# A squared-ReLU channel sub-layer: square with one operand from PSUM, plain sums in both halves, one gate near the end

## The chip, the cores and the metric

The kernel runs on one core of a Trainium2 chip, in one launch. The metric is device time in microseconds (us) of that launch. The kernel before takes 2147.57 us, the median of three runs (2147.03, 2147.57 and 2153.73).

## What is computed

One step of a decoder trunk with one layer, width D = 1024, in fp32: a prompt of 1024 rows and a sample of 8 rows share the weights. The layer has a mixer sub-layer (paged attention over a cache, gated linear attention) and a channel sub-layer. The change lies in the channel sub-layer of the prompt. For a block of rows `x1` with its modulated form `h`:

```
h   = ln(x1) * (1 + scale) + shift                # scale, shift from c
u   = h @ w_ff1                                   # 1024 x 4096
mlp = relu(u)**2 @ w_ff2                          # 4096 x 1024
y   = layer_norm(ALPHA * x1 + gate * mlp) * ln2_g + ln2_b
```

`gate` is one row of 1024 values for all rows of the prompt.

## The kernel before

The work is written as generators (flows) that yield between pieces; a planner picks the order in which instructions reach each engine, from the order of the flows, their lags and its own costs. Each engine then works through its own list strictly in order. The order around the change is thus nobody's single choice, and one changed instruction can move its neighbours on every engine.

The prompt is done in two halves of 512 rows, by `ffn(0, h2a, False)` and then `ffn(1, h2b, True)`; the second one also carries the 8 sample rows. At its start, the first runs beside the end of the paged attention of the sample (loads `kt`, `vt` by POOL, products and sums on `kt` at L659 and L661 by DVE, matmuls `va` by PE) and the norms (`xr`) of the second half's mixer.

A half has 32 units of 128 hidden columns. For each unit `up` does 24 matmuls into one of two PSUM tiles `pmm`. The factor 24 is 8 blocks of the contraction by 3 products: matmul operands are split into a high and a low part (names ending in h and l), and `three` takes high x high, low x high, high x low. Then, per unit, ACT makes `rl = relu(pmm)` (L1502), DVE squares it in place (L1503), ACT copies the high part `hidh` (L313) and DVE subtracts to get `hidl` (L314). Weights come by SP (`wf`, L319), are split by ACT (`wfh`, `wf2h`, L313) and by POOL (`wfl`, `wf2l`, L314).

Units go down in groups of two (the last group of the second half has four). A group makes 8 output tiles of 128x512, 4 row tiles `t` by 2 column halves `cc`. `down_tile` does 6 matmuls (12 for four units) into one of two PSUM tiles `pz` (cc = 0) or one of two `ptr` (cc = 1). `add_up` then brings the PSUM tile into the SBUF sum `f[t][cc]`:

- In the first half, the first group copies (DVE, L1548), later groups add (DVE, L1550). Ahead of the last group the sums are multiplied by the gate (L1614) and `ALPHA * x1`, loaded again as `xf`, is added (L1615).
- In the second half `f` is loaded with `x1` by SP in 8 transfers (L205) during the first group's `up`, and every tile of every group is gated: `tmpf = gate * pz` (L1556), then `f += tmpf` (L1560), or with ALPHA in the first group (L1558).

In both halves the last group's tiles are gated (L1556, L1560), and after each pair the norm follows: statistics on DVE (L299, L301, L304, L1630), scaling by ACT (L1632), `ln2_g` and `ln2_b` by DVE and POOL (L1633, L1634; for the last row tile of all by DVE alone, L1626, L1627), then the store (L1184). The tiles `rl`, `tmpf`, `xf` share one pool of 9 buffers.

The last sample rows (`srow`) are finished by `smp_end` beside the second half's last group.

Of the kernel before, what the change touches and what calls it, by code (L numbers as in the profile page):

```python
# [15 lines left out]
AF = mybir.ActivationFunctionType  # L16
ALU = mybir.AluOpType
# [3 lines left out]
P = 128  # L21
# [5 lines left out]
ALPHA = 2.0 ** 0.25  # L27
# [89 lines left out]
def tile_trunk_step(ctx: ExitStack, tc: tile.TileContext, i: dict, o: dict):  # L117
    nc = tc.nc
    V, S, G, E = nc.vector, nc.scalar, nc.gpsimd, nc.tensor
# [5 lines left out]
    def hk(shape, name, dt=F32):  # L125
        return sb.tile(list(shape), dt, tag="hk", name=name, bufs=N_HK)

    def mid(shape, name, dt=F32):
        return sb.tile(list(shape), dt, tag="mid", name=name, bufs=N_MID)

    def fa(shape, name, dt=F32):
        return sb.tile(list(shape), dt, tag="fa", name=name, bufs=N_FA)
# [22 lines left out]
    def p_mm(shape=(P, 512), name="pmm"):  # L155
        return ps.tile(list(shape), F32, tag="mm", name=name, bufs=2)
# [19 lines left out]
    def mm(out, lhsT, rhs, start, stop, share=1.0, **kw):  # L176

        n = 1
        for x in out.shape[1:]:
            n *= x  # L180
        if lhsT.dtype == F32R:
            tile_, dt = 0, 0.008 + n / 2286.0
        else:
            k, m = (next(x for x in (32, 64, 128) if y <= x) for y in (lhsT.shape[0], out.shape[0]))
            tile_, dt = (k, m) if k * m < P * P else 0, (0.2 + n / 610.0) * m / 128.0

        flow.t += dt * share + (0.1 if tile_ != mode[0] else 0.0)
        mode[0] = tile_
        ins = E.matmul(out, lhsT, rhs, start=start, stop=stop, **kw)  # L189
        flow.last = ins.ins.name  # L190
        flow.times.append(flow.t)
        flow.names.append(flow.last)
        return ins

    def not_before(ins, name):

        tc.add_manual_dep(
            ins.ins, name, mybir.DependencyInfo(mybir.DependencyClass.NoSync, mybir.DependencyReason.DATA),
            reason="not before the rows can be there",
        )  # L200

    def fetch(dst, src, lead):


        ins = nc.sync.dma_start(dst, src)  # L205
        x = bisect(flow.times, flow.t - lead)
        if x:
            not_before(ins, flow.names[x - 1])
# [29 lines left out]
    d_x1 = [tc.dram_tile([P, D], F32, name=f"d_x1{t}") for t in range(8)]  # L238
# [12 lines left out]
    for c in range(2):  # L251
        t = cp.tile([P, 8], F32, name=f"sel2_{c}")
# [59 lines left out]
    def split(src, hi, lo, eng=None):  # L312
        S.activation(hi, src, AF.Copy)  # L313
        (eng or G).tensor_tensor(lo, src, hi.bitcast(F32), ALU.subtract)  # L314
# [15 lines left out]
    def three(terms):  # L330

        out = []
        for a, b in ((0, 0), (1, 0), (0, 1)):
            out += [(x[a], y[b]) for x, y in terms]
        return out
# [814 lines left out]
    def rows(vec, alloc=hk):  # L1150
        out = []
        for h in range(2):
            t = alloc([P, 512], "row")
            nc.sync.dma_start(t, vec[512 * h : 512 * h + 512].partition_broadcast(P))
            out.append(t)
        return out
# [11 lines left out]
    def halves(dram, n, name, alloc=hk):  # L1168
        out = []
        for h in range(2):  # L1170
            t = alloc([n, 512], name)
            fetch(t, dram[:, 512 * h : 512 * h + 512], 0.0)
            out.append(t)
        return out
# [227 lines left out]
    def ffn(n, h2, smpl):  # L1402
# [3 lines left out]
        f = [[fa([P, 512], f"f{t}{h}") for h in range(2)] for t in range(4)]  # L1406
        yield lambda: ("h2", n) in done
        gt_t = (ada_acc, gmt.rearrange("p a b -> p (a b)"))
# [85 lines left out]
        def up(u, wh, wl):  # L1494
            p = p_mm()
            steps = three([(h2[k], (wh[:, k, :], wl[:, k, :])) for k in range(8)])
            for x, (h, wt) in enumerate(steps):
                mm(p, wt, h, start=x == 0, stop=x == 23)
                if x % 6 == 5 and x < 23:
                    yield  # L1500
            rl = hk([P, 512], "rl")
            S.activation(rl, p, AF.Relu)  # L1502
            V.tensor_tensor(rl, rl, rl, ALU.mult)  # L1503
            hid[u][0:2] = mid([P, 512], "hidh", F32R), mid([P, 512], "hidl", F32R)
            split(rl, hid[u][0], hid[u][1], V)
            yield
# [27 lines left out]
        def down_tile(us, ws, t, cc):  # L1534
            tk = slice(P * t, P * t + P)
            p = (p_z, p_tr)[cc]()
            steps = three([
                ((hid[u][0][:, tk], hid[u][1][:, tk]), (ws[x][0][:, cc, :], ws[x][1][:, cc, :]))
                for x, u in enumerate(us)
            ])  # L1540
            for x, (h, wt) in enumerate(steps):
                mm(p, h, wt, start=x == 0, stop=x == len(steps) - 1)
            return p


        def add_up(f, g, p, first):
            if n == 0 and first:
                V.tensor_copy(f, p)  # L1548
            elif n == 0:
                V.tensor_tensor(f, f, p, ALU.add)  # L1550
            else:
                gated(f, g, p, first)

        def gated(f, g, p, first=False):
            tmp = hk([P, 512], "tmpf")
            V.tensor_tensor(tmp, g, p, ALU.mult)  # L1556
            if first:
                V.scalar_tensor_tensor(f, f, ALPHA, tmp, ALU.mult, ALU.add)  # L1558
            else:
                V.tensor_tensor(f, f, tmp, ALU.add)  # L1560

        groups = [list(range(u, u + 2)) for u in range(0, NU, 2)]
        if smpl:
# [1 line left out]
        steps = [(u, None) for u in groups[0]]  # L1565
        for x, us in enumerate(groups[:-1]):
            steps += [(u, None) for u in groups[x + 1][:2]] + [(x, us)]
        us = groups[-1]
        steps += [(u, None) for u in us[2:]] + [(None, us)]

        def load(x, us):
            if us is None:
                return load_up(x)
            return (yield from load_down(us))

        def smp_end():
            yield lambda: summed == [NU // 2, NU // 2]
            part = hk([P, 512], "partf2")
            S.activation(part, pfs[0], AF.Copy)
            xs, gts = sample_rows(d_x1s, d_gate[1][1:9])  # L1580
            yield E_LAG
            for cc in range(2):
                p3 = p_tr([8, 512], "pfs3")
                mm(p3, sel2[cc], part, start=True, stop=True)
                V.tensor_tensor(gts[cc], gts[cc], p3, ALU.mult)
                V.scalar_tensor_tensor(xs[cc], xs[cc], ALPHA, gts[cc], ALU.mult, ALU.add)
            sub_ln(xs, 8, *ln2)
            store(y_s, xs, 8, nc.sync)


        ws = yield from load(*steps[0])
        for y, (x, us) in enumerate(steps[:-1]):
            if smpl and y == len(steps) - 2:
                ln2 = rows(i["ln2_g"][0]), rows(i["ln2_b"][0])
                flow.spawn(smp_end())
            nxt = yield from load(*steps[y + 1])
            if n and steps[y + 1][0] == 0 and steps[y + 1][1] is not None:
                for t in range(4):
                    for h in range(2):
                        fetch(f[t][h], d_x1[4 * n + t][:, 512 * h : 512 * h + 512], 0.0)  # L1600
            if us is None:
                yield from up(x, *ws)
            else:
                for t in range(4):
                    for cc in range(2):
                        add_up(f[t][cc], gt_t[cc], down_tile(us, ws, t, cc), x == 0)
                        yield
            ws = nxt
        us = groups[-1]
        if n == 0:  # L1610
            for t in range(4):
                xs = halves(d_x1[4 * n + t], P, "xf")
                for h in range(2):
                    V.tensor_tensor(f[t][h], f[t][h], gt_t[h], ALU.mult)  # L1614
                    V.scalar_tensor_tensor(f[t][h], xs[h], ALPHA, f[t][h], ALU.mult, ALU.add)  # L1615
        if not smpl:
            ln2 = rows(i["ln2_g"][0]), rows(i["ln2_b"][0])
        g_t, b_t = ln2
# [118 lines left out]
```

## Time and profile before

| | |
|---|---|
| device time, three runs | 2147.03, 2147.57, 2153.73 us |
| the profiled execution | 2144.41 us, span 2142.7 us |
| mean granted TensorE clock | 0.959 of full |
| PE busy | 1962.2 us (92%) |
| DVE busy | 1567.8 us (73%) |
| POOL busy | 909.5 us (42%) |
| ACT busy | 700.2 us (33%) |

Engines: PE is the matrix engine, PEld its weight loads, DVE the vector engine, ACT the scalar engine, POOL the general one, SP issues transfers. Times inside the execution are us from the start of its span. In a row of a timeline, the number in square brackets is the idle time ahead of the instruction on its own engine, and the arrow names what ended it. The channel sub-layer takes the part of the span from about 1205 us to its end. PEclk is the clock granted to PE as a share of full speed.

### The profile page before, as it was taken

Reading aid. Unit: us, or ns where it says so; the run is one execution under the profiler, and the core shown is the slowest. Engines: PE = TensorE matmul, PEld = TensorE weight load, DVE = VectorE, ACT = ScalarE, POOL = GpSimd, SP = SyncE. Lnnn points to the kernel's source line nnn. Section 1 sums busy time; section 2 is a strip of 40 time slices with the busy share of each in tenths; the row PEclk is TensorE's granted clock in tenths of the full one; section 3 lists DMA queues with packets and bytes.
Section 4 is the critical chain, followed back from the end, with each engine's and each line's share of the span. In section 5 each row is a group of like instructions: output and inputs, shape, how many; then the busy total and the mean of one; then the engine's idle time right before and its main releaser. Section 6 shows DMA issues by size and latency. Waiting matters only on the chain.

```text
span 2142.7 us, 29010 instructions
## 1 busy us (share of the span) xinstructions
PE 1962.2 (92%) x11300; PEld 1378.3 (64%) x11300; DVE 1567.8 (73%) x1882; ACT 700.2 (33%) x1136; POOL 909.5 (42%) x615
## 2 busy tenths in 40 slices
PE   5999999998999889879989789999999898999996
PEld 2776755565556656557867556676766666767774
DVE  6578898788777688567897998987436756555656
ACT  2334444543445632222232223223221332122222
POOL 2342243333334323227475647465544533233335
PEclk8999999999999879999999889999999899999998
DMA  7785678787788668898997778888667543442222
GB/s 259 253 300 189 217 244 281 241 280 245 246 277 302 214 205 293 290 340 293 330 312 278 264 258 289 279 279 303 199 216 254 177 158 119 130 136 92 87 83 85
DMA packets 270083, 498.07 MB, mean 232 GB/s; under 512 B 16005, under 2 KB 198629, under 8 KB 234106
## 3 DMA queue, kind: packets, MB, share of 16 engines
q0 software_dynamic: 36864, 268.45, 34.7%
q1 hardware_dynamic: 205538, 199.17, 29.5%
q10 hardware_dynamic: 27544, 28.59, 3.8%
q8 instruction: 89, 1.46, 0.3%
q14 instruction: 48, 0.39, 0.1%
HBM read 465.45 MB, written 30.71 MB: 232 GB/s over the span
## 4 chain that ended last, share of the span: by engine, by line
PE 54%; DVE 20%; DMA 11%; issue 8%; POOL 3%; ACT 3%; SPq 0%; DVEq 0%; ACTq 0%; POOLq 0%
PE pmm L189 20%; PE pz L189 7%; PE ptr L189 7%; PE pbig L189 7%; DMA kt<-in_cache_k,idx 4%; DVE z L661 4%; PE va L189 4%; DVE kt L659 4%; PE pfs L189 2%; DVE kp L772 1%; DMA vt<-in_cache_v,idx 1%; DMA wbr<-in_w_in 1%; DMA wf<-in_w_ff 1%; DVE st L299 1%; DMA ra<-in_w_ada 1%
## 5 line engine op out<-in xcount | busy, mean ns | idle before, releaser
L659 DVE TENSOR_TENSOR kt<-kt,qb 128x2048 f32<-128x2048 f32 x128 | 291.5, 2278 | 73.8 <-DMA kt<-in_cache_k,idx 71.6
L661 DVE TENSOR_REDUCE z<-kt 128x32 f32<-128x2048 f32 x128 | 291.6, 2280 | 1.2
L636 POOL DMA_INDIRECT vt<-in_cache_v,idx x128 | 133.2, 1041 | 309.7 <-PE va L189 133.6
L636 POOL DMA_INDIRECT kt<-in_cache_k,idx x128 | 132.7, 1037 | 283.5 <-DVE z L661 107.9
L314 POOL TENSOR_TENSOR wfl<-wf,wfh 128x1024 fp32r<-128x1024 f32 x64 | 156.4, 2444 | 206.8 <-ACT wfh L313 187.3
L314 POOL TENSOR_TENSOR wf2l<-wf,wf2h 128x1024 fp32r<-128x1024 f32 x62 | 151.3, 2440 | 117.8 <-ACT wf2h L313 105.1
L1503 DVE TENSOR_TENSOR rl<-rl 128x512 f32<-128x512 f32 x64 | 64.5, 1008 | 162.3 <-ACT rl L1502 162.2
L313 ACT ACTIVATE wfh<-wf 128x1024 fp32r<-128x1024 f32 x64 | 67.5, 1055 | 279.5 <-PE ptr L189 152.9
L189 PE MATMUL pmm<-h2h,wfh 128*128 128x512 f32 x512 | 143.9, 414 | 7.6 <-ACT rl L1502 4.3
L189 PE MATMUL va<-vt,wT 128*8 128x512 f32 x1024 | 140.7, 615 | 11.1 <-DMA vt<-in_cache_v,idx 11.0
L189 PE MATMUL pmm<-h2l,wfh 128*128 128x512 f32 x512 | 140.2, 407 | 0.5 <-POOL h2l L314 0.5
L189 PE MATMUL pmm<-h2h,wfl 128*128 128x512 f32 x512 | 133.2, 397 | 0.0
L189 PEld LDWEIGHTS pmm<-h2h,wfh 128*128 128x128 f32 x512 | 95.0, 194 | 51.4 <-issue 21.6
L189 PEld LDWEIGHTS pmm<-h2l,wfh 128*128 128x128 f32 x512 | 96.5, 192 | 31.9 <-issue 10.1
L189 PEld LDWEIGHTS pmm<-h2h,wfl 128*128 128x128 f32 x512 | 95.2, 189 | 27.2 <-issue 6.8
L1560 DVE TENSOR_TENSOR f<-f,tmpf 128x512 f32<-128x512 f32 x120 | 110.4, 943 | 1.2
L189 PE MATMUL pz<-wf2h,hidh 128*128 128x512 f32 x248 | 86.5, 414 | 21.4 <-ACT wf2h L313 10.8
L772 DVE TENSOR_TENSOR_SCAN kp<-kp,zcol 128x512 f32<-128x512 f32 (+3 forms) x96 | 99.7, 1051 | 3.6 <-ACT kp L765 2.5
L1502 ACT ACTIVATE rl<-pmm 128x512 f32<-128x512 f32 x64 | 38.2, 596 | 175.8 <-PE pmm L189 172.8
L189 PE MATMUL pz<-wf2l,hidh 128*128 128x512 f32 x248 | 83.9, 407 | 6.1 <-POOL wf2l L314 6.0
L314 DVE TENSOR_TENSOR hidl<-rl,hidh 128x512 fp32r<-128x512 f32 x64 | 75.0, 1172 | 16.8 <-ACT hidh L313 15.7
L189 PE MATMUL ptr<-wf2h,hidh 128*128 128x512 f32 x248 | 84.4, 408 | 2.0 <-DVE f L1550 1.6
(432 smaller groups left out, 4298.6 us busy)
## 6 DMA issues: line engine op xcount, KB each, us to landing
wf<-in_w_ff SPq DMA_DIRECT2D x128, 512.0 KB
ra<-in_w_ada SPq DMA_DIRECT2D x24, 1024.0 KB
wfs<-in_w_ff SPq DMA_DIRECT2D x20, 512.0 KB
wbr<-in_w_in SPq DMA_DIRECT2D x16, 512.0 KB
d_br<-brg ACTq DMA_DIRECT2D x32, 256.0 KB
g<-d_br SPq DMA_DIRECT2D x32, 256.0 KB
wo<-in_w_o SPq DMA_DIRECT2D x16, 512.0 KB
xt<-in_x_prompt SPq DMA_DIRECT2D x8, 512.0 KB
```

The source lines that it names most:

```text
L189: ins = E.matmul(out, lhsT, rhs, start=start, stop=stop, **kw)
L299: V.bn_stats(st[:n, h, :], xs[h][:n])
L313: S.activation(hi, src, AF.Copy)
L314: (eng or G).tensor_tensor(lo, src, hi.bitcast(F32), ALU.subtract)
L636: G.indirect_dma_start(t, None, src, bass.IndirectOffsetOnAxis(ap=idx[:, 16 * b + j : 16 * b + j + 1], axis=0))
L659: dot = V.tensor_tensor(k3, k3, qb[:, None, :].to_broadcast([P, 4, 512]), ALU.mult)
L661: V.tensor_reduce(z[:, :, :, j], kt.rearrange("p (r h d) -> p r h d", r=4, h=8), AX.X, ALU.add)
L772: V.tensor_tensor_scan(kp[:, 0:w][:, ::-1], kp[:, 0:w][:, ::-1], zcol.to_broadcast([P, w]), init, ALU.mult, ALU.max)
L1502: S.activation(rl, p, AF.Relu)
L1503: V.tensor_tensor(rl, rl, rl, ALU.mult)
L1560: V.tensor_tensor(f, f, tmp, ALU.add)
```

## The change

In three places:

1. The square takes one operand straight from PSUM: `relu(p) * p` instead of `relu(p) * relu(p)`. `pmm` is now released by DVE (L1503), where before ACT (L1502) released it.
2. In both halves the first group's tile is copied to `f` by ACT, and later groups are added by one DVE instruction.
3. In both halves gate and `ALPHA * x1` come once, ahead of the last group. The 8 transfers of `x1` into `f` in the second half go away; 8 transfers `xf` come at its end.

```diff
             S.activation(rl, p, AF.Relu)
-            V.tensor_tensor(rl, rl, rl, ALU.mult)
+            V.tensor_tensor(rl, rl, p, ALU.mult)
...
-        def add_up(f, g, p, first):
-            if n == 0 and first:
-                V.tensor_copy(f, p)
-            elif n == 0:
+        def add_up(f, p, first):
+            if first:
+                S.activation(f, p, AF.Copy)
+            else:
                 V.tensor_tensor(f, f, p, ALU.add)
-            else:
-                gated(f, g, p, first)
-
-        def gated(f, g, p, first=False):
+
+        def gated(f, g, p):
             tmp = hk([P, 512], "tmpf")
             V.tensor_tensor(tmp, g, p, ALU.mult)
-            if first:
-                V.scalar_tensor_tensor(f, f, ALPHA, tmp, ALU.mult, ALU.add)
-            else:
-                V.tensor_tensor(f, f, tmp, ALU.add)
+            V.tensor_tensor(f, f, tmp, ALU.add)
...
-            if n and steps[y + 1][0] == 0 and steps[y + 1][1] is not None:
-                for t in range(4):
-                    for h in range(2):
-                        fetch(f[t][h], d_x1[4 * n + t][:, 512 * h : 512 * h + 512], 0.0)
...
         us = groups[-1]
-        if n == 0:
-            for t in range(4):
-                xs = halves(d_x1[4 * n + t], P, "xf")
-                for h in range(2):
-                    V.tensor_tensor(f[t][h], f[t][h], gt_t[h], ALU.mult)
-                    V.scalar_tensor_tensor(f[t][h], xs[h], ALPHA, f[t][h], ALU.mult, ALU.add)
+        for t in range(4):
+            xs = halves(d_x1[4 * n + t], P, "xf")
+            for h in range(2):
+                V.tensor_tensor(f[t][h], f[t][h], gt_t[h], ALU.mult)
+                V.scalar_tensor_tensor(f[t][h], xs[h], ALPHA, f[t][h], ALU.mult, ALU.add)
```

Below the edit, lines have new numbers: the gated pair of the last group is L1554 and L1555, the gate block L1604 (multiply) and L1605 (with ALPHA), the norm L1616 to L1624. All instructions ahead of the first half's first group keep their order.

First place, SP's list at the first half's start, where `wf_10665` and `wf_10671` are the first group's two down weights and `x` is the second half's rows for the modulation (lines with - are before, with + after):

```order
 L319 DMA wf<-in_w_ff 128x8x128 x2
 L319 DMA wf_10665<-in_w_ff 128x1024
+L319 DMA wf_10671<-in_w_ff 128x1024
+L319 DMA wf<-in_w_ff 128x8x128
 L1381 DMA x_10783<-d_x_126 128x512
 L1381 DMA x_10786<-d_x_127 128x512
 L1381 DMA x_10789<-d_x_128 128x512
 L1381 DMA x_10792<-d_x_129 128x512
-L319 DMA wf_10671<-in_w_ff 128x1024
-L319 DMA wf<-in_w_ff 128x8x128 x2
+L319 DMA wf<-in_w_ff 128x8x128
```

The second down weight and one more weight now stand ahead of the four loads of `x`. On DVE at the same place one `hidl` (L314) now stands ahead of a product on `kt` (L659), where it stood behind it.

Second place, ACT's list at the start of the second half's first group, where `wf2h<-wf_13647` is the split of that group's second down weight:

```order
 L313 ACTIVATE hidh<-rl 128x512
 L1334 ACTIVATE partu<-pups 128x256
-L1502 ACTIVATE rl<-pmm 128x512
 L313 ACTIVATE wf2h<-wf_13647 128x1024
-L313 ACTIVATE hidh<-rl 128x512
+L1502 ACTIVATE rl<-pmm 128x512
+L313 ACTIVATE hidh<-rl 128x512
+L1548 ACTIVATE f_13498<-pz 128x512
```

The split of the weight no longer stands behind the `relu` of a later unit, and the first of the new copies follows.

Third place, DVE's list at the end of the program, from the last unit's `hidl` to the first tile of the last group. Before:

```order
L314 TENSOR_TENSOR hidl<-rl,hidh 128x512
L1585 TENSOR_TENSOR srow<-srow,pfs_16749 8x512
L1585 TENSOR_TENSOR srow<-srow,pfs_16753 8x512
L1586 SCALAR_TENSOR_TENSOR srow<-srow 8x512 x2
L299 BN_STATS st<-srow 8x6 x2
L1556 TENSOR_TENSOR tmpf<-ada_acc,pz 128x512
```

and after:

```order
L299 BN_STATS st<-srow 8x6 x2
L1605 SCALAR_TENSOR_TENSOR f_13498<-xf,f_13498 128x512
L301 BN_AGGR mv<-st 8x2
L1605 SCALAR_TENSOR_TENSOR f_13499<-xf,f_13499 128x512
L304 RECIPROCAL rs<-rs 8x1
L1605 SCALAR_TENSOR_TENSOR f_13500<-xf,f_13500 128x512
L1162 SCALAR_TENSOR_TENSOR nm<-mv,rs 8x1
L1605 SCALAR_TENSOR_TENSOR f_13501<-xf,f_13501 128x512
L1605 SCALAR_TENSOR_TENSOR f_13502<-xf,f_13502 128x512
L1165 TENSOR_TENSOR srow<-srow,row 8x512 x2
L1605 SCALAR_TENSOR_TENSOR f_13503<-xf,f_13503 128x512
L1166 TENSOR_TENSOR srow<-srow,row 8x512
```

Two more L1605 and then L1554, the first gated product, follow. All 8 instructions L1605 thus stand between the statistics of `srow` and the first tile of the last group; the 8 multiplications L1604 stand further ahead, among the tiles of the group before.

## Rows read from the trace of the kernel before

**Rows 1.** Busy time of the engines in stretches of the span (the view of stretches): for each stretch its bounds and length in us, then busy us and, in brackets, the number of instructions of PE, PEld, DVE, ACT and POOL, the granted clock of PE, the DMA share and GB/s.

```profile
1200.00:1250.00 50.00, 41.44 (x167) 29.27 (x167) 48.12 (x61) 15.80 (x27) 29.96 (x19) 0.82 0.62 211
1250.00:1300.00 50.00, 43.49 (x194) 29.37 (x193) 49.23 (x47) 12.73 (x17) 26.94 (x18) 0.93 0.85 298
1400.00:1450.00 50.00, 48.71 (x228) 35.78 (x226) 44.27 (x38) 12.62 (x16) 29.31 (x18) 1.00 0.83 291
...
1550.00:1600.00 50.00, 50.00 (x240) 35.06 (x237) 17.64 (x26) 11.68 (x15) 23.51 (x15) 1.00 0.58 201
...
1650.00:1700.00 50.00, 39.87 (x165) 29.14 (x166) 42.76 (x59) 18.89 (x28) 28.64 (x14) 0.89 0.62 188
...
2000.00:2050.00 50.00, 50.00 (x272) 36.89 (x271) 28.72 (x44) 13.30 (x17) 19.97 (x8) 1.00 0.27 85
...
2100.00:2143.00 43.00, 26.60 (x109) 18.20 (x107) 32.74 (x53) 9.27 (x16) 22.36 (x15) 0.84 0.13 50
```

**Rows 2.** All instructions of a line of the program, with shortest, median and longest duration in ns, and the start of the first and last.

```profile
L1503 DVE TENSOR_TENSOR rl<-rl x64: 665/693/2855, 1215.4 to 2104.6; 128x512 f32<-128x512 f32 x64
L1550 DVE TENSOR_TENSOR f<-f,pz x56: 661/681/690, 1276.0 to 1640.7; 128x512 f32<-128x512 f32 x56
L1556 DVE TENSOR_TENSOR tmpf<-gmt,ptr x64: 641/680/692, 1651.8 to 2130.5; 128x512 f32<-128x512 f32 x64
L1560 DVE TENSOR_TENSOR f<-f,tmpf x120: 660/689/2897, 1652.4 to 2131.2; 128x512 f32<-128x512 f32 x120
L1548 DVE COPY f<-ptr x4: 674/680/683, 1248.0 to 1261.1; 128x512 f32<-128x512 f32 x4
L1615 DVE SCALAR_TENSOR_TENSOR f<-xf,f x8: 680/682/684, 1646.4 to 1650.6; 128x512 f32<-128x512 f32 x8
L1502 ACT ACTIVATE rl<-pmm x64: 570/597/661, 1214.6 to 2104.0; 128x512 f32<-128x512 f32 x64
```

**Rows 3.** PE in order of time at the first half's start: start us, duration us, what, and the idle time ahead of it.

```profile
1232.87 0.79 PE L189 MATMUL pz<-wf2h,hidh 128*128 128x512 f32 x1 [3.93 <-ACT hidh L313]
1235.37 0.79 PE L189 MATMUL pz<-wf2h,hidl 128*128 128x512 f32 x1 [1.27 <-DVE hidl L314]
...
1270.30 0.79 PE L189 MATMUL pz<-wf2h,hidh 128*128 128x512 f32 x1 [4.83 <-ACT wf2h L313]
```

**Rows 4.** DVE in order of time, same place.

```profile
1229.00 2.85 DVE L1503 TENSOR_TENSOR rl<-rl 128x512 f32<-128x512 f32 x1
...
1232.43 2.22 DVE L659 TENSOR_TENSOR kt<-kt,qb 128x2048 f32<-128x2048 f32 x1
...
1244.83 2.53 DVE L1503 TENSOR_TENSOR rl<-rl 128x512 f32<-128x512 f32 x1
...
1263.99 2.72 DVE L1503 TENSOR_TENSOR rl<-rl 128x512 f32<-128x512 f32 x1
...
1271.62 1.67 DVE L1503 TENSOR_TENSOR rl<-rl 128x512 f32<-128x512 f32 x1
```

**Rows 5.** POOL in order of time, same place.

```profile
1228.95 2.35 POOL L314 TENSOR_TENSOR wf2l<-wf,wf2h 128x1024 fp32r<-128x1024 f32 x1
...
1254.09 1.15 POOL L636 DMA_INDIRECT vt<-in_cache_v,idx  x1 [0.31 <-DVE z L661]
```

**Rows 6.** SP's transfers in order of time: start of the first issue, us until the last one was issued, what.

```profile
1247.21 14.67 SPq L1381 DMA_DIRECT2D x<-d_x  x4
1261.98 4.58 SPq L319 DMA_DIRECT2D wf<-in_w_ff  x3
```

**Rows 7.** Busy time in shorter stretches, in the columns of group 1: after the first of PE's waits of group 3, after the third, where the second half begins, and in the tail.

```profile
1231.50:1241.70 10.20, 7.55 (x21) 5.68 (x21) 10.04 (x16) 4.88 (x8) 1.66 (x1) 0.50 0.39 134
...
1269.10:1275.90 6.80, 5.18 (x11) 3.64 (x12) 6.80 (x5) 2.63 (x3) 3.67 (x3) 0.50 1.08 360
...
1699.20:1702.60 3.40, 3.24 (x8) 2.57 (x9) 2.04 (x3) 0.00 (x0) 0.11 (x1) 0.51 0.58 170
...
2110.00:2122.00 12.00, 12.00 (x54) 9.85 (x53) 11.55 (x25) 3.92 (x7) 4.62 (x4) 1.00 0.02 3
```

**Rows 8.** PE in order of time where the second half begins.

```profile
1676.00 2.93 PE L189 MATMUL pmm<-h2h,wfh 128*128 128x512 f32 x6 [4.26 <-ACT rl L1502]
...
1696.86 0.50 PE L189 MATMUL pz<-wf2h,hidh 128*128 128x512 f32 x1 [1.17 <-ACT wf2h L313]
...
1699.36 0.80 PE L189 MATMUL pz<-wf2l,hidh 128*128 128x512 f32 x1 [1.08 <-POOL wf2l L314]
```

**Rows 9.** DVE in order of time, same place, with the square of the second half's first unit.

```profile
1678.20 1.27 DVE L1633 TENSOR_TENSOR f<-f,row 128x512 f32<-128x512 f32 x2
...
1679.51 1.64 DVE L1503 TENSOR_TENSOR rl<-rl 128x512 f32<-128x512 f32 x1
```

**Rows 10.** PE in order of time at three later places of the second half.

```profile
1728.58 0.50 PE L189 MATMUL pz<-wf2h,hidh 128*128 128x512 f32 x1 [1.14 <-ACT wf2h L313]
...
1819.67 0.50 PE L189 MATMUL pz<-wf2h,hidh 128*128 128x512 f32 x1 [2.22 <-ACT wf2h L313]
```

**Rows 11.** DVE in order of time, there and in the tail of the program.

```profile
1815.85 2.16 DVE L1503 TENSOR_TENSOR rl<-rl 128x512 f32<-128x512 f32 x1 [3.90 <-ACT rl L1502]
...
2110.19 0.66 DVE L1556 TENSOR_TENSOR tmpf<-ada_acc,pz 128x512 f32<-128x512 f32 x1
...
2135.25 3.41 DVE L1627 SCALAR_TENSOR_TENSOR f<-f,rs,row 128x512 f32<-128x512 f32 x2
```

More of the change, by code (lines that the diff above doesn't have):

```diff
@@ L1605, in ffn @@
                     for cc in range(2):
-                        add_up(f[t][cc], gt_t[cc], down_tile(us, ws, t, cc), x == 0)
+                        add_up(f[t][cc], down_tile(us, ws, t, cc), x == 0)
                         yield
```

## The prediction

> **What bounds the kernel now.** I read four views in this order. The view of stretches comes first, since it tells which engine is full where [rows 1]. Between 1400 and 2100 us PE is full or nearly so: 48.7 of 50 us at 1400, 50.0 at 1550 and at 2000. DVE has much room in the later part (17.6 of 50 at 1550, 28.7 of 50 at 2000). Three places differ. At the first half's start (1200 to 1300) DVE has 48.1 and 49.2 of 50 us and PE only 41.4 and 43.5, with a granted clock of 0.82 and 0.93. Where the second half begins (1650 to 1700) PE has 39.9 of 50. In the tail (from 2100) PE has 26.6 of 43 and DVE 32.7. So DVE work counts only at these three places and where one DVE instruction ends a PE wait.
>
> Second, the lines of DVE [rows 2]. Instructions that read PSUM are steady: `f += pz` has 661/681/690 ns, `gate * ptr` 641/680/692. Those with two SBUF sources have the same median but long ones among them: the square 665/693/2855, `f += tmpf` 660/689/2897. Third, the timelines show why: the square at 1229.00 takes 2.85 us [rows 4] and lies beside a POOL split of 2.35 us from 1228.95 [rows 5]. Fourth, PE's waits [rows 3, 8, 10] tell which of this is paid for.
>
> **The change, part by part.** The sum is made against the profiled execution, 2144.4 us, which is 3.2 us under the median of 2147.57; I put the difference on the median.
>
> *First half's start.* The square reads PSUM and should take 0.68 us, like `f += pz` [rows 2], where it took 2.85 [rows 4]. PE waited 3.93 us for the `hidh` behind it [rows 3]; 2.85 - 0.68 = 2.2 us of that go, and the rest is DVE's queue ahead of the square. The next wait, 1.27 us for `hidl` [rows 3], stood behind the 2.22 us product on `kt` [rows 4]; in the new order `hidl` goes first: -1.3. The third wait, 4.83 us for `wf2h` [rows 3], came from SP: that weight stood behind four loads of `x`, which held SP's list from 1247.21 for 14.67 us [rows 6]. Now it stands ahead: -4.8. After this wait PE ran 6.8 us at a clock of 0.50 with 5.18 us of work [rows 7], so the lower of the two levels, 1.2 GHz; without the wait the work takes half: -2.6. Together -10.9.
>
> The same from DVE: four squares (2.85, 2.53, 2.72, 1.67 [rows 4]) lose 9.77 - 2.7 = 7.1 us, and eight copies of 0.68 us [rows 2] go to ACT, 5.4 us. That is 12.5 us less on an engine with 49 of 50 us busy. The two readings agree, so I take the first, -10.9. Upper end of the gain: the first half-clock stretch, 10.2 us with 7.55 us of work [rows 7], goes as well, 3.8 more. Lower end: 0, if something else holds PE (first rival).
>
> The copies cost ACT 8 x 0.6 us (the length of its `relu` from PSUM [rows 2]) per half. ACT has 34 of 50 us free there [rows 1]: 0, if they are not queued too late (third rival).
>
> The page "Perfetto Trace Analysis" of the Trainium skill, section "Optimizing Scalar/DVE Operations", speaks against the new square: it gives DVE about 60 ns of access overhead for SBUF and about 125 for PSUM. By that figure each of 64 squares would be 65 ns dearer, an estimate of 0.26 us for the four at the start, and the sum would be 0.3 us smaller. The medians above show no such surcharge: 681 ns with PSUM, 689 without [rows 2].
>
> *Second half's beginning.* Here the change adds a wait. The third unit's matmuls need the first unit's `pmm` back. It was released by the `relu`, and PE started at 1676.00 after 4.26 us of waiting [rows 8]. Now the square releases it, and that one stands on DVE behind the norms of the first half's last rows, at 1679.51 [rows 9]. With 0.68 us it ends at 1680.2: +4.2, and what is queued behind it on PE shifts with it. Against it, the waits of 1.17 us for `wf2h` and 1.08 for `wf2l` [rows 8] should go, since that split no longer stands behind a `relu` on ACT: -2.2. The half-clock stretch after them, 3.4 us with 3.24 of work [rows 7], gives -1.6. Sum +0.4, bounds -4 (the norms run earlier too) and +5 (nothing is won back). The eight transfers of `x1` that leave SP here delayed nothing else that I see: 0.
>
> *Second half's groups.* 112 products `gate * tile` go, 8 additions move to ACT, and 16 DVE instructions come: 104 x 0.68 = 71 us less on DVE. PE is full there, 50.0 of 50 [rows 1]: 0. Two waits are touched: 1.14 us for `wf2h` at 1728.58, which now stands ahead of `hidh` on ACT, and 2.22 us at 1819.67 [rows 10], which hangs on a square of 2.16 us at 1815.85 [rows 11]. The latter loses 2.16 - 0.68 = 1.5. Together -2.6, bounds 0 and -3.4. The 8 multiplications of the gate block lie among PE-bound tiles with DVE at 29 of 50 [rows 1]: 0; without that cover they would cost 5.5.
>
> *Tail.* Eight instructions with ALPHA now stand on DVE between the `srow` statistics and the last group's first `tmpf`, at 2110.19 [rows 11]. From there DVE works nearly without a pause (11.55 of the next 12 us [rows 7]) until its last instruction ends at 2138.7 [rows 11], and the last stores hang on that. So they count in full: 8 x 0.682 [rows 2] = +5.5. No row shows their transfers `xf` landing at this place. Lower end +2, if PE's last tiles set the pace (PE, too, is full in those 12 us); upper end +8, if one transfer is late or POOL stretches one to the 2.9 us of the longest in group 2.
>
> Sum: -10.9 + 0.4 - 2.6 + 5.5 = **-7.6 us**: 2136.8 for an execution like the profiled one, **2140.0** against the median.
>
> **The rivals.**
>
> *The start's gain is given back (no change).* The products `va` in PE's list need `vt`, and POOL issues that only once DVE's sum over a `kt` has freed a buffer, as at 1254.09 [rows 5]. If these loads set the pace, PE comes 11 us early and waits. For it: DVE has 44.3 of 50 at 1400 [rows 1]. Against it: DVE itself is relieved by 12.5 us. Result +0.4 - 2.6 + 5.5 plus what is kept of the gain: 0 to +3, about 2149.
>
> *The square stays long.* If POOL also holds instructions with one PSUM source, 2.2 and 1.5 us of the sum fall away: -3.9, 2143.7. Against it stand the two lines that read PSUM, with no duration over 692 ns [rows 2]; for it nothing but the changed kind of operands.
>
> *ACT holds the first group (slower).* ACT's list runs in order, and the eight copies stand among `relu`, splits and store issues, some of which wait for POOL. PE's fifth tile needs the first copy. If ACT comes to a copy later than PE to the tile that needs its buffer, PE waits, 0.6 us and more per tile; 8 such waits are 5 us, and the gain of 10.9 at the start never appears. Result +0.4 - 2.6 + 5.5 + 5 = +8.3: 2155.9. It decides from the point where copies come later than the DVE copies came before, from 1248.0 to 1261.1 [rows 2]. Against it: ACT has 34 of 50 us free.
>
> *More than forecast.* The first half-clock stretch goes too (-3.8) and the norms before the second half run 4 us earlier, so that the added wait vanishes: -15.4, 2132.2.
>
> **How the numbers follow.** A measurement of this kernel can tell about 0.3%, 6.4 us, from no change: the limits are 2141.1 and 2154.0. Forecast 0.50, with its own range 2135 to 2144, 0.35 of it beyond 2141.1. Gain given back 0.22, of which 0.04 ends over 2154. Square stays long 0.05. ACT holds the first group 0.13, slower. More than forecast 0.10. So faster 0.35 + 0.10 = 0.45, slower 0.13 + 0.04 = 0.17, same 0.38. From 2131 to 2153 lie the forecast, the no-change cases and half of the best case; most of the slower case and the other half are left out, under 0.2.
>
> **What would show it.** Right, if the square's longest duration falls to about 0.7 us; PE's waits at the start (3.93, 1.27, 4.83) shrink to under 3 us in all; PE waits about 8 us for `rl` of L1503 where the second half begins; the first `tmpf` of the last group starts 5 to 6 us later against PE's preceding matmuls. Wrong, if PE's busy share from 1200 to 1300 stays at 85 of 100 us, if a wait on a copy of ACT heads PE's waits, or if waits on `vt` appear between 1250 and 1450.

## The result and the profile after

The changed kernel takes 2132.92 us (median of five runs, 2129.62 to 2137.19) against 2147.57 before; the ratio is 0.9925, with a 95% interval of 0.9901 to 0.995. The profiled execution took 2129.62 us with a span of 2127.9. The forecast was 2140.0, in 2131 to 2153: the sign and the range held, but the gain is 14.6 us where 7.6 were forecast.

The view of stretches, at the places of [rows 1]:

```profile
1200.00:1250.00 50.00, 42.50 (x182) 29.36 (x180) 46.28 (x66) 20.75 (x34) 32.50 (x21) 0.87 0.71 238
1250.00:1300.00 50.00, 46.08 (x214) 32.52 (x214) 45.28 (x43) 15.16 (x23) 30.42 (x20) 0.97 0.86 299
...
1650.00:1700.00 50.00, 42.28 (x201) 30.79 (x204) 32.73 (x51) 23.12 (x35) 30.65 (x15) 0.93 0.46 146
...
2000.00:2050.00 50.00, 50.00 (x273) 37.08 (x271) 16.65 (x29) 13.51 (x18) 18.32 (x8) 1.00 0.26 79
...
2100.00:2128.00 28.00, 11.93 (x46) 9.30 (x44) 23.67 (x37) 5.74 (x10) 17.91 (x12) 0.75 0.20 76
```

At the start PE has 3.7 us more in the first 100 and the clock is higher in both stretches; in the steady part PE is as full as before, while DVE falls from 28.7 to 16.7 of 50. The lines of the change, as in [rows 2]:

```profile
L1503 DVE TENSOR_TENSOR rl<-rl,pmm x64: 629/686/690, 1216.8 to 2085.9; 128x512 f32<-128x512 f32 x64
L1550 DVE TENSOR_TENSOR f<-f,pz x108: 622/687/690, 1272.0 to 2065.0; 128x512 f32<-128x512 f32 x108
L1548 ACT ACTIVATE f<-pz x8: 579/596/602, 1237.8 to 1702.6; 128x512 f32<-128x512 f32 x8
L1605 DVE SCALAR_TENSOR_TENSOR f<-xf,f x16: 627/676/682, 1641.5 to 2097.7; 128x512 f32<-128x512 f32 x16
```

No square is longer than 0.69 us; the copies cost ACT 0.6 us each. PE and DVE at the first half's start, which answer to [rows 3, 4]:

```profile
1229.23 3.32 PE L189 MATMUL pmm<-h2h,wfh 128*128 128x512 f32 x8 [4.22 <-DVE rl L1503]
...
1270.37 1.58 PE L189 MATMUL va<-vt,wT 128*8 128x512 f32 x8 [2.97 <-DMA vt<-in_cache_v,idx]
```

```profile
1228.52 0.66 DVE L1503 TENSOR_TENSOR rl<-rl,pmm 128x512 f32<-128x512 f32 x1
...
1230.80 0.68 DVE L314 TENSOR_TENSOR hidl<-rl,hidh 128x512 fp32r<-128x512 f32 x1
```

The waits of 1.27 us for `hidl` and 4.83 for `wf2h` are gone. The one of 3.93 for `hidh` is not: PE waits 4.22 us for the same square, now because it releases `pmm`. A wait of 2.97 us for `vt` is new. PE and DVE where the second half begins, which answer to [rows 8, 9]:

```profile
1668.92 1.05 PE L189 MATMUL posT<-ones,vz 128*128 128x1 f32 x8 [2.07 <-DVE vz L738]
1674.14 3.37 PE L189 MATMUL pmm<-h2h,wfh 128*128 128x512 f32 x8 [4.17 <-DVE osT L743]
1677.34 2.02 PE L189 MATMUL pmm<-h2l,wfh 128*128 128x512 f32 x8
...
1690.53 0.50 PE L189 MATMUL pz<-wf2l,hidh 128*128 128x512 f32 x1 [0.95 <-POOL wf2l L314]
```

```profile
1673.36 0.63 DVE L1503 TENSOR_TENSOR rl<-rl,pmm 128x512 f32<-128x512 f32 x1
1673.91 0.15 DVE L743 COPY osT<-posT 128x4 f32<-128x4 f32 x1
```

PE starts the third unit right after that square (the row names the small instruction behind it). And the tail, as in [rows 11]:

```profile
2090.33 1.27 DVE L299 BATCH_NORM_STATS2 st<-srow 8x6 f32<-8x512 f32 x2
2091.53 0.66 DVE L1605 SCALAR_TENSOR_TENSOR f<-xf,f 128x512 f32<-128x512 f32 x1
...
2098.35 0.67 DVE L1554 TENSOR_TENSOR tmpf<-ada_acc,pz 128x512 f32<-128x512 f32 x1
...
2120.45 3.41 DVE L1617 SCALAR_TENSOR_TENSOR f<-f,rs,row 128x512 f32<-128x512 f32 x2
```

The first `tmpf` comes 8.0 us after the start of the `srow` statistics; before it followed them at once.

**A steadier measure.** The first relu (L1502) starts between 1206.9 and 1222.0 us in the profiles below, although all that is ahead of it is the same program. So beside the times each kernel is given by parts of its profile from the first relu of the channel sub-layer: "stage" is from there to the end of the span, "tail" from the last relu to that end. "Idle" sums the gaps between PE's matmul records from the first relu to the last; "low" is the time in that stretch at a granted clock of 0.5 (1.2 of 2.4 GHz), with PE's busy time in it behind the slash, about half of which the lower level costs. Each ratio is against the kernel before as timed beside it (medians of 2146.2 to 2146.4 us in the experiments), and it is not the quotient of the two medians, which for the changed kernel is 0.9932.

| kernel | median us | ratio, 95% | stage | idle | low | tail |
|---|---|---|---|---|---|---|
| before | 2147.57 | | 928.1 | 41.4 | 41.0 / 35.5 | 38.7 |
| before again (e11) | 2149.37, one run | | 927.5 | 42.9 | 34.1 / 31.1 | 38.8 |
| changed | 2132.92 | 0.9925 (0.9901 to 0.995) | 911.8 | 33.3 | 17.1 / 13.0 | 42.6 |
| changed again (e7) | 2132.25 | 0.9929 (0.9907 to 0.9952) | 914.3 | 32.3 | 27.3 / 22.0 | 43.2 |
| e1 square only | 2139.69 | 0.9968 (0.9951 to 0.9984) | 921.8 | 36.7 | 44.4 / 35.9 | 38.7 |
| e2 sums only | 2147.93 | 1.001 (0.9991 to 1.0029) | 922.8 | 38.1 | 27.3 / 23.2 | 42.6 |
| e3 gate early | 2128.01 | 0.9921 (0.9903 to 0.994) | 906.1 | 28.9 | 23.9 / 19.6 | 39.0 |
| e4 DVE load back | 2131.85 | 0.9946 (0.9925 to 0.9966) | 911.7 | 32.8 | 20.5 / 14.8 | 43.2 |
| e5 copies on DVE | 2140.93 | 0.9959 (0.9935 to 0.9983) | 921.7 | 33.9 | 41.0 / 34.6 | 43.2 |
| e6 early release | 2142.02 | 0.9977 (0.9961 to 0.9993) | 919.4 | 33.7 | 30.7 / 29.4 | 42.5 |
| e8 e3 and e6 | 2143.03 | 0.9975 (0.9952 to 0.9998) | 911.2 | 34.9 | 17.1 / 13.9 | 38.7 |
| e9 gate each tile | 2134.6 | 0.9928 (0.99 to 0.9957) | 912.7 | 34.4 | 27.3 / 21.5 | 38.8 |
| e10 gate early again | 2131.5 | 0.9933 (0.9904 to 0.9961) | 909.7 | 32.3 | 23.9 / 18.2 | 39.5 |

Two profiles of one kernel differ by 0.6, 2.5 and 3.6 us in the stage. A profile is of one execution: that of e4 took 11.5 us less than the median of its kernel, that of e8 9.5, that of e5 5.6 and that of e2 5.1. Where stage and ratio disagree, the ratio rests on more runs.

### The profile page after: what moved, and what is told of

Read it like the earlier page. It is cut to its first block, busy times and chain, and to the rows that moved or that the text cites. A ratio compares the mean times of both kernels' runs of the same rounds, so it can differ in the third digit from the quotient of the medians.

```text
span 2127.9 us, 28882 instructions
## 1 busy us (share of the span) xinstructions
PE 1954.9 (92%) x11300; PEld 1372.5 (64%) x11300; DVE 1460.7 (69%) x1770; ACT 709.9 (33%) x1152; POOL 909.7 (43%) x615
## 3 DMA queue, kind: packets, MB, share of 16 engines
q0 software_dynamic: 36864, 268.45, 34.9%
## 4 chain that ended last, share of the span: by engine, by line
PE 49%; DVE 18%; DMA 14%; issue 11%; POOL 4%; ACT 3%; SPq 0%; DVEq 0%; ACTq 0%; POOLq 0%
PE pmm L189 21%; PE pz L189 7%; PE ptr L189 7%; DMA kt<-in_cache_k,idx 5%; DVE z L661 3%; PE pbig L189 3%; PE va L189 3%; DVE kt L659 3%; PE pfs L189 2%; DMA vt<-in_cache_v,idx 2%; DVE kp L772 2%; DMA wo<-in_w_o 1%; DMA wbr<-in_w_in 1%; DMA wf<-in_w_ff 1%; DVE xr L1299 1%
## 5 line engine op out<-in xcount | busy, mean ns | idle before, releaser
L659 DVE TENSOR_TENSOR kt<-kt,qb 128x2048 f32<-128x2048 f32 x128 | 291.5, 2278 | 80.9 <-DMA kt<-in_cache_k,idx 78.1
L314 POOL TENSOR_TENSOR wfl<-wf,wfh 128x1024 fp32r<-128x1024 f32 x64 | 155.4, 2429 | 206.2 <-ACT wfh L313 187.5
L314 POOL TENSOR_TENSOR wf2l<-wf,wf2h 128x1024 fp32r<-128x1024 f32 x62 | 150.6, 2430 | 113.7 <-ACT wf2h L313 91.2
L1503 DVE TENSOR_TENSOR rl<-rl,pmm 128x512 f32<-128x512 f32 x64 | 43.7, 682 | 134.8 <-ACT rl L1502 134.5
L1550 DVE TENSOR_TENSOR f<-f,pz 128x512 f32<-128x512 f32 x108 | 73.9, 684 | 70.5 <-PE pz L189 69.3
L189 PEld LDWEIGHTS pmm<-h2l,wfh 128*128 128x128 f32 x512 | 95.2, 189 | 31.1 <-issue 9.7
L1550 DVE TENSOR_TENSOR f<-f,ptr 128x512 f32<-128x512 f32 x108 | 73.9, 684 | 44.2 <-PE ptr L189 43.5
L189 PE MATMUL pz<-wf2h,hidh 128*128 128x512 f32 x248 | 83.5, 405 | 10.9 <-DVE tmpf L1554 4.5
L1502 ACT ACTIVATE rl<-pmm 128x512 f32<-128x512 f32 x64 | 38.2, 597 | 164.5 <-PE pmm L189 161.1
L314 DVE TENSOR_TENSOR hidl<-rl,hidh 128x512 fp32r<-128x512 f32 x64 | 79.0, 1234 | 15.9 <-ACT hidh L313 15.7
```

What stands on the lines that cost most here:

```text
L659: dot = V.tensor_tensor(k3, k3, qb[:, None, :].to_broadcast([P, 4, 512]), ALU.mult)
L1503: V.tensor_tensor(rl, rl, p, ALU.mult)
```

## The experiments

**e1 and e2, the two edits apart.** e1 is the kernel before with the new square; e2 is the changed kernel with the old one (this edit the other way round).

```diff
-            V.tensor_tensor(rl, rl, rl, ALU.mult)
+            V.tensor_tensor(rl, rl, p, ALU.mult)
```

> The kernel before with one edit, the square's second operand from PSUM; sums and gate as before. Theory A (the gain comes from the square, which no longer gets long, and from the order of the lists that the planner then writes, so from waits of PE; less DVE work is worth nothing): most of the gain at the start and in the transition shows, and there is no price in the tail, so 6 to 12 us faster than before (about 2138), the squares at 0.69 us at most, PE's 4.8 us wait for wf2h gone, a wait of about 4 us for the square's release of pmm in its place at the start. Theory B (the gain comes from the DVE work that plain sums save, 71 us in the second half and 5 at each first group): within 3 us of before.

> The changed kernel with the square in its old form (both operands from SBUF); copies on ACT, plain sums and one gate as changed. Theory A: the wait for the long square at the start stays (3.9 us), wf2h's wait of 4.8 us goes, the tail costs 4 to 5 us, so 2 to 6 us faster than before (about 2143); squares up to 2.9 us long. Theory B: 12 to 16 us faster than before, like the changed kernel.

e1 gains 0.32% and 6 us of stage, as theory A says. e2 gains 5 us of stage, which the tail has already taken 4 from, but nothing in the times, where theory A had 2 to 6 us; its longest square has 3158 ns. Theory B falls in its simple form, since the sums alone don't give the gain. By parts (relus numbered from 0; before and changed are means of two profiles), the start, relu 0 to 7, takes 86.8 us before, 84.6 in e1, 80.8 in e2 and 79.4 changed, so most of its gain comes with the sums. Relu 35 to 40 takes 88.1, 85.1, 84.3 and 81.2: there the two add up. From relu 40 to 63 it is 321.2, 316.9, 317.0 and 317.3: there either edit gives all. The times show more together (0.73%) than apart (0.32% and nothing). The stages, 6.0 + 5.0 = 11 us apart and 14.7 together, differ by hardly more than two profiles of one kernel do, and they don't tell where the two help each other. PE's waits at the start (1212 to 1310 us; what was waited for, us in all, times, longest) show e1 trading one wait for others:

```profile
PE pmm L189 <- DVE rl L1503: 4.2, 1, 4.2
PE pz L189 <- DVE f L1550: 2.9, 1, 2.9
PE va L189 <- DMA vt<-in_cache_v,idx: 2.1, 1, 2.1
```

**e5, who copies.** In the changed kernel the first group's copy goes back to DVE in both halves.

```diff
             if first:
-                S.activation(f, p, AF.Copy)
+                V.tensor_copy(f, p)
```

> The changed kernel with the first group's copies on DVE in place of ACT, in both halves. From the first relu to the end of the span it took 928.1 us before and 911.8 changed; the two edits apart gave 921.8 and 922.8, so 4.7 us came only with both. Theory A (the copies on ACT, which free a full DVE at the two first groups, make these 4.7 us and a part of the start): 915 to 919 us from the first relu to the end, 3 to 7 us slower than the changed kernel. Rival D (copies on ACT are worth nothing; square, order and plain sums do it): 910.5 to 913 us, within 1.5 us of the changed kernel.

The stage is 921.7 us, 7 to 10 more than the changed kernel, and the ratio is worse, though its interval still touches that of the changed kernel: theory A, and more than it expected. But of the two first groups that it names only the first half's shows a gain: relu 0 to 7 takes 84.7 us (changed kernel 78.4 and 80.5), while relu 35 to 40, with the second half's first groups, takes 82.0 (80.6 and 81.8). PE's timeline has the e1 wait again:

```profile
1275.18 1.22 PE L189 MATMUL pz<-wf2h,hidh 128*128 128x512 f32 x2 [2.96 <-DVE f L1550]
```

DVE, in order of time, comes late to that addition, behind a sum on `kt` and a long `hidl`:

```profile
1268.82 2.28 DVE L661 TENSOR_REDUCE z<-kt 128x32 f32<-128x2048 f32 x1
1271.01 3.52 DVE L314 TENSOR_TENSOR hidl<-rl,hidh 128x512 fp32r<-128x512 f32 x1
1274.45 0.68 DVE L1550 TENSOR_TENSOR f<-f,pz 128x512 f32<-128x512 f32 x1
```

The idle time is that of the changed kernel within 2 us (33.9); the loss shows at the lower clock, 34.6 us of PE work where the changed kernel has 13.0 and 22.0.

**e4, DVE's load in the second half.** One unused product ahead of each plain addition of the second half:

```diff
             else:
+                if n:
+                    V.tensor_tensor(hk([P, 512], "tmpf"), gt_t[0], p, ALU.mult)
                 V.tensor_tensor(f, f, p, ALU.add)
```

> The changed kernel with one more product gate times tile on DVE ahead of each of the 104 plain additions of the second half, its result unused: the DVE work of before comes back, order and gate as changed. Theory A (DVE's load in the second half is worth nothing, since PE is full): 0 to 3 us slower than the changed kernel (about 2134.5). Theory B (the saved DVE work is the gain there): 8 to 12 us slower (about 2143).

The groups of DVE's lines in the second half show the load back:

```profile
L1551 DVE TENSOR_TENSOR tmpf<-ada_acc,ptr 128x512 f32<-128x512 f32 x52 | 35.5, 683 | 4.1 <-PE ptr L189 3.6
L1551 DVE TENSOR_TENSOR tmpf<-ada_acc,pz 128x512 f32<-128x512 f32 x52 | 35.4, 681 | 34.0 <-PE pz L189 33.3
```

That is 70.9 us of DVE work, and the stage is 911.7 us, the changed kernel's within 3; from relu 35 to 63 it takes 397.0 us, the changed kernel 397.1 and 400.1. So they are worth nothing there, as theory A and the prediction have it. The times are less sharp: the ratio is 0.2% worse, with an interval that lies over the changed kernel's.

**e9, gate each tile of the second half.** The new square, ACT's copies in the first half, and the second half's sums as before (an edit of the kernel before):

```diff
-            V.tensor_tensor(rl, rl, rl, ALU.mult)
+            V.tensor_tensor(rl, rl, p, ALU.mult)
...
             if n == 0 and first:
-                V.tensor_copy(f, p)
+                S.activation(f, p, AF.Copy)
```

> The changed square in both halves and the copies on ACT in the first half; the second half in the old form (x1 loaded into f, every tile gated, no block near the end). All lists are those of the changed kernel up to the second half's first groups. Theory A (gating once is worth nothing in the steady part, gains about 4 us at the second half's first groups, where a DVE copy or gate stood in PE's way, and costs 3.9 us in the tail): from the first relu to the end 910 to 915 us, the part from relu 35 to relu 40 about 85 us (80.6 and 81.8 in the changed kernel), the tail from the last relu 38.7 us; in all the same as the changed kernel within 3 us. Theory B (the gate is where the gain is): 918 us or more.

Stage 912.7, the changed kernel's (911.8, 914.3); ratio 0.9928 against 0.9925 and 0.9929. From relu 35 to relu 40 (counted from 0) it took 85.1 us, in the changed kernel 80.6 and 81.8, before 88.1 and 88.2; the tail 38.8, 42.9 in the mean of the changed kernel's. All as expected: in the second half, plain sums and one gate gain 4 us at the first groups and lose 4 in the tail. (The copies on ACT have no share in those 4 that shows: with copies on DVE, in e5, the part takes 82.0.) For this kernel that part of the change is worth nothing as it stands.

**e3 and e10, the gate block early.** It goes right behind the last plain sums, ahead of the last two units' `up`; `gate_block` holds the five lines taken out below:

```diff
                         add_up(f[t][cc], down_tile(us, ws, t, cc), x == 0)
                         yield
+                if us is groups[-2]:
+                    gate_block()
...
         us = groups[-1]
-        for t in range(4):
-            xs = halves(d_x1[4 * n + t], P, "xf")
-            for h in range(2):
-                V.tensor_tensor(f[t][h], f[t][h], gt_t[h], ALU.mult)
-                V.scalar_tensor_tensor(f[t][h], xs[h], ALPHA, f[t][h], ALU.mult, ALU.add)
```

> The changed kernel with the gate block (gate, then ALPHA times the loaded rows) of the second half right behind the last plain sums, ahead of the last two units' up, in place of behind them. Theory A (the eight additions with ALPHA between the sample row's statistics and the last tiles delay the tail by about 4 us): 3.5 to 5 us faster than the changed kernel (about 2128.5), PE's wait of 1.8 us in the last group gone. Rival C (the tail is set by POOL and the stores, whatever stands on DVE ahead of it): within 1 us of the changed kernel.

> The kernel with the gate block ahead of the last two units' up once more, to tell it from the changed kernel. Theory A: tail of 39.0 us from the last relu to the end (42.6 and 43.2 in the changed kernel), 905 to 910 us from the first relu to the end, 4 us faster than the changed kernel in the median. If the first run was chance: 912 us or more.

In e3's timeline of DVE the additions with ALPHA now fill DVE's pause ahead of the last units, and `tmpf` follows the statistics at once:

```profile
2066.92 3.09 DVE L1591 SCALAR_TENSOR_TENSOR f<-xf,f 128x512 f32<-128x512 f32 x5
...
2088.31 1.27 DVE L299 BATCH_NORM_STATS2 st<-srow 8x6 f32<-8x512 f32 x2
2089.50 0.66 DVE L1554 TENSOR_TENSOR tmpf<-ada_acc,pz 128x512 f32<-128x512 f32 x1
```

The tail falls from 42.6 and 43.2 to 39.0 and 39.5, and the stage to 906.1 and 909.7, the lowest of all. Rival C falls. The kernel beats the one before (0.9921 and 0.9933). That it beats the changed one the times don't show: the intervals lie over each other, and e10's median, 2131.5, is only 1 us lower, where 4 were expected; the profiles alone show it, by 3.6 us in the tail (the means).

**e6 and e8, early release of `pmm`.** The old square in the first two units of each half, in the changed kernel (e6) and in e3 (e8):

```diff
-            V.tensor_tensor(rl, rl, p, ALU.mult)
+            V.tensor_tensor(rl, rl, rl if u < 2 else p, ALU.mult)
```

> The changed kernel with the old square (both operands from SBUF) in the first two units of each half only, so that ACT releases their pmm as before; all other squares read PSUM. Theory A (releasing pmm late costs PE about 4.2 us at the start and 2 us more than before in the transition, while the long square costs about the same at the start): the wait for the release of pmm at the start goes, a wait of 3 to 4 us for hidh comes in its place, the transition wait falls from 6.2 to about 4.3 us; in all 0 to 3 us faster than the changed kernel. Rival E (what the square gives at the start is most of that stretch's gain): 4 us or more slower.

> Gate block ahead of the last two units' up, and the old square in the first two units of each half. Theory A: the gains of both add, 904 to 907 us from the first relu to the end (906.1 with the early gate alone), 2125 to 2129 us in all. Rival E: 908 us or more, slower than the early gate alone.

The waits went as theory A had it. From 1210 to 1310 us of e6, and from 1655 to 1700:

```profile
PE pz L189 <- ACT hidh L313: 4.0, 1, 4.0
PE ptr L189 <- DVE f L1550: 2.7, 1, 2.7
...
PE pz L189 <- DVE hidl L314: 1.3, 1, 1.3
```

```profile
PE pmm L189 <- ACT rl L1502: 4.3, 2, 3.4
PE pz L189 <- ACT wf2h L313: 1.2, 1, 1.2
PE pz L189 <- POOL wf2l L314: 1.1, 1, 1.1
```

Yet e6 is slower, by 5 to 8 us of stage and 10 to 11 us by the ratios, and e8, against e3 and e10, by 2 to 5 us of stage and 9 to 12 by the ratios: rival E. e6 loses 3 us from relu 0 to 7 (82.6 against 79.4) and 3 from relu 35 to 40 (84.4 against 81.2). With the old square the waits for `hidl` and `wf2h` are back, because the planner again writes the old order, with `hidl` behind the product on `kt` and the weight's split behind a relu (the wait for `wf2l` is 0.95 us in the changed kernel too). So the late release is no net loss: what comes with the new square outweighs it. My theory on this point was wrong.

**e7 and e11, the same kernels again.**

> The changed kernel once more, for its profile and its times beside the others of this call. If the lower clock's share repeats: the stretches at the lower clock between the first and the last relu sum to 14 to 24 us (17 in the first profile, 41 before), 911 to 914 us from the first relu to the end, and 2130 to 2136 us in all. If the clock's share was chance: they sum to 30 us or more, and the stretch takes 917 us or more.

> The kernel before once more, for a second profile. If its share of the lower clock repeats: 35 to 45 us at the lower clock between the first and the last relu, 926 to 930 us from the first relu to the end. If that was chance: under 30 us and under 923 us.

Neither hit its band of the lower clock: the changed kernel had 27.3 us (14 to 24 expected, 30 if chance), the one before 34.1 (35 to 45). So its share varies from run to run by 7 to 10 us, and still lies 7 us apart between the kernels at the nearest. The stages repeat: 927.5 as expected, 914.3 against an expected upper end of 914.

## Why the forecast held, and where its steps failed

By the relus (numbered from 0), with the mean of two profiles on each side:

| part | forecast | before | changed | measured |
|---|---|---|---|---|
| relu 0 to 7, the start | -10.9 | 86.8 | 79.4 | -7.4 |
| relu 7 to 31 | 0 | 326.0 | 326.7 | +0.7 |
| relu 31 to 35, the added wait | +4.2 | 66.9 | 65.5 | -1.4 |
| relu 35 to 63 | -6.4 | 409.4 | 398.6 | -10.8 |
| tail | +5.5 | 38.8 | 42.9 | +4.1 |
| sum | -7.6 | | | -14.8 |

*The start* was forecast too large, and for reasons of which half held. `hidl` and `wf2h` no longer stop PE (1.3 and 4.8 us), as forecast; the wait for `wf2h` goes with either edit alone (none left in e1, 0.8 us in e2). But the 2.2 us on the square's own wait did not come: I had seen that the square now releases `pmm` where the second half begins, and not that the same holds at the start. A part of the first rival came too: PE waits 3.5 and 4.3 us for `vt` in the two profiles. In place of these, ACT's copies gave what the first reading of the sum had at 0: without them the same part takes 84.7 us (e5). The reading from DVE, full there at 49 of 50, was the better one in kind, though not in size (12.5 us): a copy that leaves a full engine counts even if PE doesn't wait for the copy itself.

*The added wait* is the step that failed most. It is there: PE starts the third unit 4.9 us after the second half's first relu (1669.2 us), where it was 0.6 us after it (1675.4), so 4.3 later, as forecast. It cost nothing: PE's idle time from relu 31 to 35 is 8.1 and 9.7 us in the two profiles before and 8.9 and 9.4 in the changed kernel's. The sum put 4.2 us on top of the 4.26 that PE waited here already, 8 to 9 us in all. Measured are 2.07 and 4.17 us (the first two rows of PE above), with the small `posT` matmuls between them, which before stood inside the unit; and the wait of 1.09 us for `partu` behind them is gone. In the first profile the lower clock overlapped the wait as well; the stretch at 0.50, in the columns of [rows 7]:

```profile
1670.10:1676.90 6.80, 2.76 (x7) 2.21 (x8) 4.41 (x10) 3.26 (x5) 4.92 (x4) 0.50 0.41 139
1676.90:1695.00 18.10, 17.15 (x85) 12.28 (x84) 8.99 (x11) 8.87 (x15) 9.35 (x5) 1.00 0.48 154
```

PE had 2.76 us of work in it. Before, the lower level lasted from 1675.3 to 1685.5 with 9.50 us of work. This did not repeat: from relu 31 to 35 PE had 5.8 us of work at the lower level in e7 and 6.1 in e11. So the -1.4 of the table owes something to the first two profiles; that the added wait cost nothing is the safe reading.

*The second half's groups.* That 71 us less on DVE are worth nothing in the steady part was right (e4). The waits for `wf2h` that I priced moved as said: 1.17 and 1.14 us are gone, 2.22 is 0.64 and 0.91. The first group's wait for `wf2l`, 1.08 us, was to go and stayed, at 0.95 and 0.62. I had left out PE's waits behind gated tiles, 0.46 and 2.62 us for L1556, of which 1.92 for a plain sum is left, and the lower clock in this part: from relu 35 to 63 PE had 9.8 and 10.2 us of work at it before, none and 6.7 in the changed kernel. From relu 35 to 40 the square alone gives 3 us (e1 and e9, 85.1) and the plain sums 4 more.

*The tail*: 5.5 forecast, 4.1 measured, by the mechanism named (the early gate takes 3.6 of it away).

*The clock* is the mis-sized term: 4.2 us were put on it. PE's idle time from relu 0 to 63 fell from 42.2 to 32.8, 9.4 us, where the forecast's waits sum to 8.9. (As a sum only: the single waits came out otherwise, see above.) Half of PE's work at the lower level fell from 16.7 to 8.8 us, 7.9. The two sum to 17.3 of the 18.9 us between those relus; what is left, 1.6, I can't assign. The 7.9 is a mean of profiles that vary: by single profiles it lies between 4.5 and 11.2. Nor does it follow the idle time alone: e1 and e5 idle 5.5 and 8.3 us less than the kernel before and have as much work at the lower level as that (35.9 and 34.6 us).

*The rivals.* No copy of ACT heads PE's waits, so the slower case did not come, and squares are short. "More than forecast" said -15.4 for a shorter lower clock at the start and an added wait that vanishes. The first came in part (3.4 us at 0.50 where 10.2 were), the second in effect. Of the signs that I named, the short squares came; PE's waits at the start did not shrink to under 3 us (the release of `pmm` alone takes 4.22), and a wait on `vt`, a sign of being wrong, did appear. That the range held is in part luck: the start fell 3.5 us short of the forecast, and the added wait and the second half's groups gave 10.0 us more than it.

On the square the Trainium skill's page "Perfetto Trace Analysis", section "Optimizing Scalar/DVE Operations", would have it 65 ns dearer with PSUM, an estimate from its two overheads; the medians are 686 ns with, 693 without, so the trace does not agree.

## What to carry to other kernels

Price an engine's relief by the stage: 71 us off DVE were worth nothing where PE was full, and eight copies of 0.68 us off a DVE that was full were worth about their length (5.3 us from relu 0 to 7, e5 against the changed kernel). When an edit lets a later instruction release a buffer, look at every place where the next user waits for it. And count the clock with the waits: between these two kernels PE's waits fell by 9.4 us and the cost of the lower level by 7.9, though how much varies from run to run, and e1 and e5 lost waits without that second gain.

## What was not expected of the hardware

The contention of POOL and DVE also runs the other way. One POOL instruction on 8 x 512 elements took 1.67 us before; in the changed kernel's tail, beside the train of additions with ALPHA (two SBUF sources each), it took 4.06 (the first row is from before):

```profile
2114.43 1.67 POOL L1166 TENSOR_TENSOR srow<-srow,row 8x512 f32<-8x512 f32 x1 [11.47 <-DVE srow L1165]
2095.49 4.06 POOL L1166 TENSOR_TENSOR srow<-srow,row 8x512 f32<-8x512 f32 x1 [11.69 <-DVE srow L1165]
```

Only the store of the sample rows waited for it. All six profiles with the gate block at this place have 4.06 or 4.07 us, the seven others, e3 and e10 among them, 1.67 or 1.68. It ends at 2099.55, when DVE's last addition with ALPHA is done (2098.42) and two gated products with one source in PSUM have followed. The Trainium skill's page "SBUF — State Buffer", section "SBUF: two separate sides", names such a pair: a DVE instruction with two SBUF inputs and a POOL instruction that reads SBUF share a port pair as an exclusive lock. The traces agree: squares with two SBUF sources reach 2855 and 3158 ns, and of the 64 that read PSUM none passes 690.
